# Products of a token block joined in halves of the contraction, and one rotation of eight PSUM banks for the FFN

## The chip, the cores and the metric

The kernel runs on one core of a Trainium2 chip. The time is the device time in microseconds (us) of one execution of the whole program, taken as the median of three runs. The profile shows one execution by engine: TensorE (PE, its weight loads as PEld), VectorE (DVE), ScalarE (ACT), GpSimd (POOL), and the queues of DMA issues, of which SyncE's (SP) and ScalarE's carry most here.

## The reference

One layer of a diffusion backbone: 2048 latent tokens of width 1024, and 256 context tokens beside them.

```python
n = modulate(rmsnorm(h, g), shift, scale)                 # for latent and context tokens
q, k, v, u, gate_attn, gate_ssm = split(n @ w_in)         # one in-projection
a = neighbourhood_attention(rope(q), rope(k), v, k_ctx, v_ctx, rpb)   # 8 heads of 64
s = s5_branch(u_ctx, u)                                   # bidirectional complex-diagonal scan
h = h + g1 * ((sigmoid(gate_attn) * (a @ w_branch_attn)
             + sigmoid(gate_ssm) * (s @ w_branch_ssm)) @ w_out)
h = h + g2 * swiglu(modulate(rmsnorm(h, g_ffn), sh2, sc2))  # hidden width 2816
out = rmsnorm(h, final_g)

def swiglu(h):
    a, b = split(h @ w_ffn_in)
    return (silu(a) * b) @ w_ffn_out
```

All inputs are float32. The kernel keeps float32 by splitting each operand in a high and a low part (`hi`, `lo`) and adding three products, hi x hi, hi x lo and lo x hi.

## The kernel before

**Stages.** The program runs the norm of all tokens (`norm_u`, which also stores the normalised tokens, split in two, to DRAM as `ns`), then the S5 scan and the attention with the in-projection running beside both, then the merge of the two branches, and from about 1800 us on the FFN. Tokens go in four blocks of 512.

**What sets the order.** The code is written operation by operation, and a scheduler puts the instructions of each engine in an order by priorities and by a timeline that it simulates. Code inside `hot()` has a higher priority (L64 to L66); the whole in-projection has a lower one, so that its products fill what the scan leaves. Each engine and each DMA queue then runs its own list strictly in order, and an instruction that waits holds up all behind it on its engine. Buffers come from pools with a fixed number of slots; a new tile waits for the readers of the old one.

**Weights.** `piece` (L79) loads a weight tile of 512 KB (`raw`, issued by SP at L76), lets ScalarE write its high part (`whi`, L70) and VectorE its low part (`wlo`, L71). `mm3` (L89 to L94) issues the three matmuls of one contraction tile: L92, L93 and L94.

**In-projection** (`in_proj`, L350). For blocks 1 to 3 the eight tiles of normalised tokens (`n`, each 128 x 2 x 512) are loaded from `ns` on SP's queue (L357), into a ring of 12 slots that the old block's tiles and the tables of the attention's bias (`biases`, L430, on GpSimd, in block 1) also use. A block runs the four k products (`qk`, `isk` true), v, the four q products and 2 x 8 gate products, all through `cols` (L96), which takes one weight piece at a time and adds 8 contraction tiles x 3 matmuls of 512 columns onto one PSUM bank. The pool `gpm` has two banks. The results of q and k go through rotary products on ScalarE and VectorE into `qt` (two slots, written at L397 and L398), which `store` (L362) sends out in four DMAs on SP's queue.

**FFN** (`ffn`, L1096). Each block has 11 pairs of calls of `ffn_in` (L1019), one call for the half `a` of the hidden units and one for `b`. A call computes a 256 x 512 result (two halves of the units by two halves of the tokens) by Strassen's scheme in Winograd's form: seven products of 12 matmuls each, with 256 columns (`prod`, L1063 to L1069), instead of eight. The weight side of the products is named s1, s3, s2, s4, a11, a22, a12; s1 and s3 share one split weight (`s13`), s2 and s4 another (`s24`), a11 and a22 a third (`r[0]`), and a12 has its own. The sums `s13` (block 0 only) and `s24` are made by GpSimd (L1036, L1037, L1049, L1050), and later blocks load `s13` from DRAM. The token side, `X`, has seven tiles for each of four contraction tiles.

A call has two PSUM banks, `pa` and `pb`, each with two halves of 256 columns, out of a pool of four (`fpm`). The products leave their sums there, and VectorE and ScalarE read them: L1076 copies s1's result, L1079 adds s3's to it, L1084 and L1085 read a11's and s2's, L1087 reads s4's, L1090 a22's, L1093 a12's. A wait for a bank is a wait for the readers of both of its halves.

After three or four pairs (a group) the products with `w_f2` follow (L92 to L94 by `product`, L1158): two column halves of 512, each with four token tiles `j` in four banks `pos` of their own pool `po`. In the last group of a block GpSimd and VectorE turn the sums into the output, and the next block's tokens are normalised and transposed meanwhile: `norm_ffn` (L990) has four steps, each with transposes into two banks out of `fpm`, and per step two rounds of VectorE and ScalarE work (L1010 to L1016) that make `X` out of `os`. One step is taken after each weight piece (`between`).

## Time and profile before

| | |
|---|---|
| median of three runs | 3296.73 us (3295.64 to 3303.11) |
| the profiled execution | 3294.7 us, its span 3292.9 us |
| busy share of the span | PE 95%, PEld 83%, DVE 70%, ACT 49%, POOL 27% |
| mean granted clock of TensorE | 0.983 of full |
| the chain that ended last | PE 72%, DVE 11%, DMA 9%, the rest 8% |

The span is what the trace covers; the 1.8 us around it belong to the execution. A busy share is a mean over all stages. A row of the waits says which engine and line waited, for which engine and line, how long in total, how often and how long at most. A matmul row's own length is longer than the distance to the next start, since matmuls are pipelined.

### The profile page before, as it was taken

How to read it: one execution, taken by the hardware profiler on the slowest of the kernel's cores; microseconds unless marked ns; L12 is line 12 of the kernel's file. 1: busy time of each engine (PE TensorE's matmuls, PEld its weight loads, DVE VectorE, ACT ScalarE, POOL GpSimd, SP SyncE). 2: the span in 40 equal slices, each digit the busy share in tenths (PEclk: the TensorE clock that was granted, in tenths of full speed). 3: DMA queues.
4: the chain of work that ended last, by engine and by line, in shares of the span. 5: the costliest groups of instructions: out<-in, count | busy, mean ns of one | idle time of the engine just before them, and what ended most of it. 6: DMA issues, size and time to landing. Idle time of an engine off the chain costs nothing.

```text
span 3292.9 us, 54200 instructions
## 1 busy us (share of the span) xinstructions
PE 3140.3 (95%) x20600; PEld 2738.5 (83%) x20600; DVE 2313.2 (70%) x4121; ACT 1598.6 (49%) x2778; POOL 882.4 (27%) x856
## 2 busy tenths in 40 slices
PE   8999978999899999899999999999999999999998
PEld 6987766777788778778898888889989898989988
DVE  6688787888353475565657766887869856886666
ACT  4455434554465545456553444444535543554534
POOL 2000052001232222223200444632241423442242
PEclk9999989999999999999999999999999999999999
DMA  8445566445776887786847334434344333343332
GB/s 333 171 122 168 170 203 221 164 140 165 231 210 189 243 267 231 225 261 191 259 145 243 131 129 137 138 128 144 113 139 146 121 116 130 134 149 130 107 112 100
DMA packets 212852, 564.27 MB, mean 171 GB/s; under 512 B 31784, under 2 KB 63656, under 8 KB 212592
## 3 DMA queue, kind: packets, MB, share of 16 engines
q1 hardware_dynamic: 155008, 437.48, 40.1%
q0 software_dynamic: 28032, 87.64, 9.8%
q10 hardware_dynamic: 29552, 35.70, 3.2%
q8 instruction: 162, 2.65, 0.3%
q14 instruction: 98, 0.80, 0.1%
HBM read 446.95 MB, written 111.61 MB: 170 GB/s over the span
## 4 chain that ended last, share of the span: by engine, by line
PE 72%; DVE 11%; DMA 9%; issue 3%; ACT 2%; POOL 2%; SPq 0%; ACTq 0%; DVEq 0%; POOLq 0%
PE ps L92 10%; PE ps L94 10%; PE ps L93 10%; PE ps L1067 6%; PE ps L1069 6%; PE ps L1068 6%; PE po L93 4%; PE po L92 4%; PE po L94 4%; DVE wlo L71 4%; PE o L924 3%; DMA raw<-in_w_m 2%; DMA n<-in_rpb 2%; PE w L884 2%; PE w L905 1%
## 5 line engine op out<-in xcount | busy, mean ns | idle before, releaser
L71 DVE TENSOR_TENSOR wlo<-raw,whi 128x1024 fp32r<-128x1024 f32 (+1 forms) x522 | 661.5, 1269 | 350.1 <-ACT whi L70 341.3
L70 ACT CAST whi<-raw 128x1024 fp32r<-128x1024 f32 (+1 forms) x522 | 507.6, 974 | 536.0 <-PE ps L1068 141.5
L1067 PE MATMUL ps<-X,whi 128*128 128x256 f32 x2464 | 700.0, 285 | 30.8 <-DVE u L1085 10.6
L1069 PE MATMUL ps<-X,wlo 128*128 128x256 f32 x2464 | 689.9, 285 | 10.0 <-DVE wlo L71 8.6
L1068 PE MATMUL ps<-X,whi 128*128 128x256 f32 x2464 | 694.4, 283 | 0.0
L1067 PEld LDWEIGHTS ps<-X,whi 128*128 128x128 f32 x2464 | 471.7, 191 | 42.2 <-DVE u L1085 16.2
L1069 PEld LDWEIGHTS ps<-X,wlo 128*128 128x128 f32 x2464 | 465.8, 191 | 17.9 <-DVE wlo L71 17.9
L1068 PEld LDWEIGHTS ps<-X,whi 128*128 128x128 f32 x2464 | 471.8, 191 | 1.3
L92 PE MATMUL ps<-n,whi 128*128 128x512 f32 (+1 forms) x800 | 321.5, 402 | 32.0 <-DVE t L384 17.6
L93 PE MATMUL ps<-n,whi 128*128 128x512 f32 (+1 forms) x800 | 318.4, 398 | 0.0
L94 PE MATMUL ps<-n,wlo 128*128 128x512 f32 (+1 forms) x800 | 317.5, 398 | 0.0
L93 PE MATMUL po<-wlo,zh 128*128 128x512 f32 x704 | 277.6, 394 | 0.0
L94 PE MATMUL po<-whi,zl 128*128 128x512 f32 x704 | 275.6, 394 | 0.0
L92 PE MATMUL po<-whi,zh 128*128 128x512 f32 x704 | 270.4, 394 | 0.0
L92 PEld LDWEIGHTS ps<-n,whi 128*128 128x128 f32 x800 | 152.6, 191 | 73.0 <-DVE t L384 14.7
L1049 POOL TENSOR_TENSOR os<-raw 128x512 f32<-128x512 f32 x66 | 96.2, 1457 | 391.6 <-DMA raw<-in_w_f 364.2
L1050 POOL TENSOR_TENSOR os<-raw,os 128x512 f32<-128x512 f32 x88 | 147.0, 1670 | 190.4 <-DMA raw<-in_w_f 188.2
L71 DVE TENSOR_TENSOR wlo<-os,whi 128x1024 fp32r<-128x1024 f32 x110 | 149.2, 1356 | 60.8 <-ACT whi L70 60.6
L70 ACT CAST whi<-os 128x1024 fp32r<-128x1024 f32 x110 | 115.3, 1048 | 143.8 <-POOL os L1050 41.9
L94 PEld LDWEIGHTS ps<-n,wlo 128*128 128x128 f32 x800 | 152.7, 191 | 36.3 <-issue 3.5
L93 PEld LDWEIGHTS ps<-n,whi 128*128 128x128 f32 x800 | 153.1, 191 | 33.7 <-issue 2.1
L92 PE MATMUL ps<-y,whi 128*128 128x512 f32 x384 | 157.1, 410 | 10.4 <-DVE t L968 5.1
(341 smaller groups left out, 7101.7 us busy)
## 6 DMA issues: line engine op xcount, KB each, us to landing
raw<-in_w_f SPq DMA_DIRECT2D x198, 512.0 KB
raw<-sums SPq DMA_DIRECT2D x66, 512.0 KB
raw<-in_w_gate SPq DMA_DIRECT2D x64, 512.0 KB
raw<-in_w_f SPq DMA_DIRECT2D x66, 256.0 KB
raw<-in_w_qk SPq DMA_DIRECT2D x32, 512.0 KB
gsc<-e ACTq DMA_DIRECT2D x64, 256.0 KB
raw<-in_w_m SPq DMA_DIRECT2D x32, 512.0 KB
t<-gsc SPq DMA_DIRECT2D x64, 256.0 KB
```

The costliest lines, as they stand in the source:

```text
L70: self.nc.scalar.copy(hi, x)
L71: self.nc.vector.tensor_tensor(lo, x, hi.bitcast(F32), op=ALU.subtract)
L92: mm(ps, l[0], r[0], start=first, stop=False)
L93: mm(ps, l[0], r[1], start=False, stop=False)
L94: mm(ps, l[1], r[0], start=False, stop=last)
L884: nc.tensor.matmul(slv, q[:, qs], kl, start=(n == 0), stop=(n == 1))
L924: nc.tensor.matmul(o[h, g, :, hf, :], l, r, start=(n == 0), stop=(n == nb + 1), skip_group_check=True)
L1049: nc.gpsimd.tensor_tensor(s24[:, 0], s13[:, 0], a11, op=ALU.subtract)
L1050: nc.gpsimd.tensor_tensor(s24[:, 1], a12, s24[:, 0], op=ALU.subtract)
L1067: mm(dst, a[0][:, k], xh, start=(first and k == 0), stop=False, skip_group_check=True)
L1068: mm(dst, a[0][:, k], xl, start=False, stop=False, skip_group_check=True)
L1069: mm(dst, a[1][:, k], xh, start=False, stop=(k == 3), skip_group_check=True)
```

## The change

In the in-projection, `cols` takes a number `pair`: the two products that begin there get both weights and both PSUM banks at once, and run tiles 0 to 3 of the contraction for the one and the other, then tiles 4 to 7 for the one and the other. It is used for the last two gate products of blocks 0 to 2 and for the first two k products of blocks 1 to 3.

In the FFN the four banks of `fpm` and the four of `fpo` become one rotation of eight. A call of `ffn_in` takes four of them, one for each of its sums, and uses half of each; a step of `norm_ffn` takes two, a column half of the `w_f2` products four. The products of a call are written in the order s1, s3, a11, s2, s4, a22, a12, s3's now begins its bank anew, and `fu` has three slots instead of two.

```diff
@@ -93,12 +93,24 @@
         mm(ps, l[0], r[1], start=False, stop=False)
         mm(ps, l[1], r[0], start=False, stop=last)
 
-    def cols(self, pool, src, kt, c0, n, ops, tag="ps"):
+    def cols(self, pool, src, kt, c0, n, ops, tag="ps", pair=None):
 
 
 
         nm = 8 // kt
         for c in range(n):
+            if pair is not None and c == pair:
+                f = ops[0][1]
+                ws = [self.piece(src, 0, c0 + c + i, kt) for i in range(2)]
+                pss = [pool.tile([P, ops[0][0]], F32, name=tag) for _ in range(2)]
+                for h in range(2):
+                    for w, ps in zip(ws, pss):
+                        for k in range(h * kt // 2, (h + 1) * kt // 2):
+                            self.mm3(ps, (w[0][:, k], w[1][:, k]), f(k), k == 0, k == kt - 1)
+                for i, ps in enumerate(pss):
+                    yield c + i, 0, ps
+            if pair is not None and c in (pair, pair + 1):
+                continue
             w = self.piece(src, 0, c0 + c, kt)
             for m in range(nm):
                 sl = slice(m * P, (m + 1) * P)
@@ -368,7 +380,7 @@
                         nc.sync.dma_start(dst[:, j, d, h, :, t:t + n].rearrange("i r t -> r i t"), x[p:p + 32].bitcast(F32))
 
             def qk(c0, ops, isk):
-                for jj, i, ps in self.cols(pm, I["w_qk"], KD, c0, 4, ops):
+                for jj, i, ps in self.cols(pm, I["w_qk"], KD, c0, 4, ops, pair=0 if b and isk else None):
                     with self.hot():
                         qt = ev.tile([P, 2, TB], F32R, name="qt")
                         if i:
@@ -420,7 +432,7 @@
                                               e[r * 64 + hf * 24:r * 64 + hf * 24 + 40])
             qk(0, [lat], False)
             for gi in range(2):
-                for m, _, ps in self.cols(pm, I["w_gate"], KD, gi * 8, 8, [lat]):
+                for m, _, ps in self.cols(pm, I["w_gate"], KD, gi * 8, 8, [lat], pair=6 if gi and b < NB - 1 else None):
                     g = ev.tile([P, TB], F32, name="e")
                     with self.hot():
                         nc.scalar.activation(g, ps, AF.Tanh, scale=0.5)
@@ -1057,8 +1069,7 @@
                 self.split(hi.rearrange("p a k m -> p a (k m)"), lo.rearrange("p a k m -> p a (k m)"), x)
             ops += [(hi[:, i], lo[:, i]) for i in range(x.shape[1])]
         s1, s3, s2, s4, a11, a22, a12 = ops
-        pa = pm.tile([P, 2, 256], F32, name="ps")
-        pb = pm.tile([P, 2, 256], F32, name="ps")
+        pb1, pb0, pa1, pa0 = (pm.tile([P, 2, 256], F32, name="ps")[:, 0] for _ in range(4))
 
         def prod(dst, a, x, first=True):
             for k in range(4):
@@ -1071,26 +1082,28 @@
         c = [tp.tile([P, 2, 256], F32, name="n") for _ in range(2)]
         u = up.tile([P, 256], F32, name="u")
         v = up.tile([P, 256], F32, name="u")
-        prod(pb[:, 1], s1, 3)
+        prod(pb1, s1, 3)
         with self.hot():
-            nc.scalar.copy(v, pb[:, 1])
-        prod(pb[:, 0], s3, 5, False)
+            nc.scalar.copy(v, pb1)
+        prod(pb0, s3, 5)
         with self.hot():
-            V.tensor_tensor(v, pb[:, 0], v, op=ALU.add)
-        prod(pa[:, 1], s2, 4)
-        prod(pb[:, 1], s4, 2, False)
-        prod(pa[:, 0], a11, 0, False)
+            V.tensor_tensor(v, pb0, v, op=ALU.add)
+        prod(pa0, a11, 0)
         with self.hot():
-            nc.scalar.copy(u, pa[:, 0])
-            V.tensor_tensor(u, pa[:, 1], u, op=ALU.add)
+            nc.scalar.copy(u, pa0)
+        prod(pa1, s2, 4)
+        with self.hot():
+            V.tensor_tensor(u, pa1, u, op=ALU.add)
             V.tensor_tensor(c[1][:, 1], u, v, op=ALU.add)
-            V.tensor_tensor(c[0][:, 1], pb[:, 1], u, op=ALU.add)
-        prod(pb[:, 0], a22, 6, False)
+        prod(pb1, s4, 2, False)
         with self.hot():
-            V.tensor_tensor(c[1][:, 0], pb[:, 0], u, op=ALU.add)
-        prod(pa[:, 0], a12, 1, False)
+            V.tensor_tensor(c[0][:, 1], pb1, u, op=ALU.add)
+        prod(pb0, a22, 6, False)
         with self.hot():
-            nc.scalar.copy(c[0][:, 0], pa[:, 0])
+            V.tensor_tensor(c[1][:, 0], pb0, u, op=ALU.add)
+        prod(pa0, a12, 1, False)
+        with self.hot():
+            nc.scalar.copy(c[0][:, 0], pa0)
         return [x.rearrange("p a t -> p (a t)") for x in c]
 
     def ffn(self, xs_, os, xp, tp, pm, first):
@@ -1102,11 +1115,11 @@
             ap = self.pool("fa", 4, ctx)
             wp = self.pool("fw", 4, ctx)
             hp = self.pool("fh", 1, ctx)
-            up = self.pool("fu", 2, ctx)
+            up = self.pool("fu", 3, ctx)
             os = Rotation(os, 2, self.pool("fos2", 1, ctx), 1)
             self.wr = Rotation(self.wr, 2, self.pool("fwr", 2, ctx), 2)
             self.wh = Rotation(self.wh, 3, self.pool("fwh", 1, ctx), 1)
-            po = self.pool("fpo", 4, ctx, space=PSUM)
+            pm = Rotation(pm, 4, self.pool("fpo", 4, ctx, space=PSUM), 4)
             fg = cp.tile([P, D], F32, name="fg")
             nc.sync.dma_start(fg, I["fg"].partition_broadcast(P))
             nxt = first
@@ -1163,7 +1176,7 @@
 
                     for c in range(2):
                         cs = slice(c * 512, c * 512 + 512)
-                        pos = {j: po.tile([P, 512], F32, name="po") for j in range(4)}
+                        pos = {j: pm.tile([P, 2, 256], F32, name="ps").rearrange("p a t -> p (a t)") for j in range(4)}
                         if last and end:
                             ws = [self.piece(I["w_f2"], m2, c, 2) for m2 in range(p0, p1)]
                         else:
```

The lists of TensorE show it inside a call of block 0 (`ps` are the PSUM banks, `X0` to `X3` the token side, `whi` and `wlo` the weight, whose numbers go up by four from s13 to s24, r[0] and r[1]). Before: whi_20646 is s13, whi_20650 s24 and whi_20654 r[0] of one call, whi_20781 s13 of the next. The piece begins with the end of a11.

```order
L1069 MATMUL ps_20662<-X2_17800,wlo_20655 128x256
L1067 MATMUL ps_20662<-X3_17801,whi_20654 128x256
L1068 MATMUL ps_20662<-X3_17801,whi_20654 128x256
L1069 MATMUL ps_20662<-X3_17801,wlo_20655 128x256
L1067 MATMUL ps_20663<-X0_17798,whi_20650 128x256 [waits DVE_49]
L1068 MATMUL ps_20663<-X0_17798,whi_20650 128x256
L1069 MATMUL ps_20663<-X0_17798,wlo_20651 128x256
L1067 MATMUL ps_20663<-X1_17799,whi_20650 128x256
L1068 MATMUL ps_20663<-X1_17799,whi_20650 128x256
L1069 MATMUL ps_20663<-X1_17799,wlo_20651 128x256
L1067 MATMUL ps_20663<-X2_17800,whi_20650 128x256
```

s4 goes onto ps_20663, the bank of s1 and s3, directly behind a11, and waits for VectorE (`DVE_49`): s3 was left there two products earlier (before s2 and a11), and L1079 has to have read it. After, in a call of the same block (whi_20535 is s13, whi_20539 s24, whi_20543 r[0]):

```order
L1078 MATMUL ps_20554<-X0_17798,whi_20543 128x256 [waits Activation_49]
L1079 MATMUL ps_20554<-X0_17798,whi_20543 128x256
L1078 MATMUL ps_20553<-X0_17798,whi_20539 128x256
L1079 MATMUL ps_20553<-X0_17798,whi_20539 128x256
L1080 MATMUL ps_20553<-X0_17798,wlo_20540 128x256 [waits DVE_49]
L1078 MATMUL ps_20553<-X1_17799,whi_20539 128x256
L1080 MATMUL ps_20554<-X0_17798,wlo_20544 128x256 [waits DVE_49]
L1078 MATMUL ps_20554<-X1_17799,whi_20543 128x256
L1079 MATMUL ps_20554<-X1_17799,whi_20543 128x256
L1080 MATMUL ps_20554<-X1_17799,wlo_20544 128x256
```

a11 begins behind s3 and takes turns with s2, each on a bank of its own. The place at which s4 begins:

```order
L1080 MATMUL ps_20553<-X2_17800,wlo_20540 128x256
L1078 MATMUL ps_20553<-X3_17801,whi_20539 128x256
L1079 MATMUL ps_20553<-X3_17801,whi_20539 128x256
L1080 MATMUL ps_20553<-X3_17801,wlo_20540 128x256
L1078 MATMUL ps_20551<-X0_17798,whi_20539 128x256 [waits Activation_49]
L1079 MATMUL ps_20551<-X0_17798,whi_20539 128x256
L1080 MATMUL ps_20551<-X0_17798,wlo_20540 128x256
L1078 MATMUL ps_20551<-X1_17799,whi_20539 128x256
```

s4 goes onto ps_20551, where s1 was left three products earlier, and waits for ScalarE (`Activation_49`) instead of VectorE.

In the in-projection, at the start of block 1, TensorE's list before (n_6558 to n_6565 are the block's tokens, whi_6666 the first k weight, whi_6711 the second, `py` belongs to the scan):

```order
L94 MATMUL ps_6670<-n_6562,wlo_6667 128x512
L92 MATMUL ps_6670<-n_6563,whi_6666 128x512 [waits DMAHW2_49]
L93 MATMUL ps_6670<-n_6563,whi_6666 128x512
L782 MATMUL py_3204<-cl_2916,h110_3198 128x8x16 [waits DVE_49]
L780 MATMUL py_3204<-mt_2967,ug_2890 128x8x16
L781 MATMUL py_3204<-cl_2916,h101_3151 128x8x16
L782 MATMUL py_3204<-cl_2916,h111_3201 128x8x16 [waits DVE_49]
L94 MATMUL ps_6670<-n_6563,wlo_6667 128x512
L92 MATMUL ps_6670<-n_6564,whi_6666 128x512 [waits DMAHW4_49]
L93 MATMUL ps_6670<-n_6564,whi_6666 128x512
L94 MATMUL ps_6670<-n_6564,wlo_6667 128x512
L92 MATMUL ps_6715<-n_6558,whi_6711 128x512 [waits Activation_49]
```

The first k product goes through all eight tiles before the second begins. After (whi_6672 is the second weight):

```order
L92 MATMUL ps_6676<-n_6563,whi_6666 128x512 [waits DMAHW2_49]
L93 MATMUL ps_6676<-n_6563,whi_6666 128x512
L94 MATMUL ps_6676<-n_6563,wlo_6667 128x512
L92 MATMUL ps_6677<-n_6558,whi_6672 128x512 [waits Activation_49]
L93 MATMUL ps_6677<-n_6558,whi_6672 128x512
L94 MATMUL ps_6677<-n_6558,wlo_6673 128x512 [waits DVE_49]
```

The second product begins after the first product's tile 3, and tile 4 follows only after it has gone through its own four:

```order
L92 MATMUL ps_6677<-n_6561,whi_6672 128x512
L93 MATMUL ps_6677<-n_6561,whi_6672 128x512
L94 MATMUL ps_6677<-n_6561,wlo_6673 128x512
L92 MATMUL ps_6676<-n_6564,whi_6666 128x512 [waits DMAHW3_49]
L93 MATMUL ps_6676<-n_6564,whi_6666 128x512
L94 MATMUL ps_6676<-n_6564,wlo_6667 128x512
```

So tile 4 of the new block, and each load wait behind it, stands 12 matmuls later. (What is called a tile's number here is its place among the eight, counted from 0; the scheduler has put some tiles in another order.)

SP's queue near the end of the same block (`n_7820` and `n_7821` are the first tiles of block 2, `qs` the stored q), before:

```order
L76 DMA raw_7344<-in_w_gate 128x1024 [waits DMAHW2_49,DMAHW0_49,DVE_49]
L368 DMA qs_78<-qt_7119 32x2x512 [waits DMAHW3_49,DVE_49]
L368 DMA qs_78<-qt_7119 32x2x512 [waits DMAHW4_49]
L368 DMA qs_78<-qt_7119 32x2x512
L368 DMA qs_78<-qt_7119 32x2x512 [waits DMAHW6_49]
L76 DMA raw_7378<-in_w_gate 128x1024 [waits DMAHW7_49,DMAHW1_49,DVE_49]
L357 DMA n_7820<-ns_85 128x1024 [waits DMASW1_49,DMASW0_49,Pool_49]
L357 DMA n_7821<-ns_85 128x1024 [waits DMASW6_49,DMASW7_49,DMASW5_49,DMASW4_49]
```

After:

```order
L76 DMA raw_7344<-in_w_gate 128x1024 [waits DMAHW2_49,DMAHW0_49,DVE_49]
L369 DMA n_7820<-ns_85 128x1024 [waits DMASW3_49,DMASW4_49,DMASW2_49,DMASW5_49,DMASW1_49,DMAHW3_49,DMASW0_49,Pool_49]
L380 DMA qs_78<-qt_7119 32x2x512 [waits DMAHW4_49,DVE_49]
L380 DMA qs_78<-qt_7119 32x2x512 [waits DMAHW5_49]
L380 DMA qs_78<-qt_7119 32x2x512 [waits DMAHW6_49]
L380 DMA qs_78<-qt_7119 32x2x512
L369 DMA n_7821<-ns_85 128x1024 [waits DMASW6_49,DMASW5_49,DMASW4_49]
L76 DMA raw_7378<-in_w_gate 128x1024 [waits DMAHW1_49,DVE_49]
```

The load of n_7820, which waits for GpSimd, now stands ahead of the four stores of qt_7119 and of the gate weight raw_7378.

## Rows read from the trace of the kernel before

**Rows 1.** Waits of PE, FFN: engine line waited for: us in total, times, longest

```profile
PE ps L1067 <- DVE u L1085: 10.6, 11, 3.2
PE ps L1067 <- DVE u L1079: 10.5, 11, 1.6
PE ps L1069 <- DVE wlo L71: 8.6, 13, 1.9
PE ps L1067 <- ACT u L1076: 3.8, 2, 2.1
PE ps L1067 <- DVE n L1087: 2.8, 3, 1.6
```

**Rows 2.** The same, token block 0

```profile
PE ps L1067 <- DVE u L1079: 10.2, 10, 1.6
PE ps L1069 <- DVE wlo L71: 6.1, 7, 1.9
```

**Rows 3.** Single matmuls of PE: start us, length us, what it is

```profile
2641.20 0.28 PE L1067 MATMUL ps<-X,whi 128*128 128x256 f32 x1
2641.32 0.28 PE L1068 MATMUL ps<-X,whi 128*128 128x256 f32 x1
...
2644.74 0.39 PE L92 MATMUL po<-whi,zh 128*128 128x512 f32 x1
2644.97 0.39 PE L93 MATMUL po<-wlo,zh 128*128 128x512 f32 x1
```

**Rows 4.** Stretches of one pair: us, busy (instructions) by engine, PEclk, DMA, GB/s

```profile
1973.45:1996.51 23.06, 21.16 (x170) 20.34 (x169) 21.20 (x26) 12.08 (x19) 13.41 (x8) 1.00 0.45 149
2829.99:2850.82 20.83, 20.30 (x171) 20.10 (x169) 17.68 (x25) 11.96 (x19) 7.49 (x4) 1.00 0.38 127
```

**Rows 5.** Groups of VectorE, first stretch: count, busy us, mean ns, idle before

```profile
L1126 DVE SCALAR_TENSOR_TENSOR n<-n 128x512 f32<-128x512 f32 x3 | 3.6, 1190 | 0.0
```

**Rows 6.** The same, second stretch

```profile
L71 DVE TENSOR_TENSOR wlo<-os,whi 128x1024 fp32r<-128x1024 f32 x2 | 2.4, 1220 | 0.5 <-ACT whi L70 0.5
...
L1126 DVE SCALAR_TENSOR_TENSOR n<-n 128x512 f32<-128x512 f32 x2 | 1.4, 675 | 0.0
```

**Rows 7.** Groups of ScalarE, second stretch

```profile
L70 ACT CAST whi<-os 128x1024 fp32r<-128x1024 f32 x3 | 3.2, 1052 | 3.7 <-POOL os L1050 2.5 <-PE ps L1069 1.3
```

**Rows 8.** Single matmuls of PE where block 1 ends, idle before in brackets

```profile
2577.09 0.39 PE L1067 MATMUL ps<-X,whi 128*128 128x256 f32 x1 [2.06 <-ACT u L1076]
...
2581.98 0.41 PE L1067 MATMUL ps<-X,whi 128*128 128x256 f32 x1 [3.19 <-DVE u L1085]
```

**Rows 9.** Tile os on VectorE: durations in ns, least, median, longest

```profile
L1010 DVE TENSOR_SCALAR os<-ps,A,B x32: 526/535/541, 1719.1 to 2906.5; 128x256 f32<-128x256 f32 x32
L1012 DVE TENSOR_TENSOR os<-os x32: 274/282/1377, 1720.0 to 2910.4; 128x128 f32<-128x128 f32 x32
...
L71 DVE TENSOR_TENSOR X<-os,X x32: 1072/1084/1952, 1723.9 to 2921.0; 128x896 fp32r<-128x896 f32 x32
```

**Rows 10.** Group of GpSimd, whole run

```profile
L1188 POOL TENSOR_TENSOR acc<-acc,n 128x512 f32<-128x512 f32 x28 | 40.1, 1441 | 143.6 <-DVE n L1186 143.6
```

**Rows 11.** Waits of PE, 300 to 900 us

```profile
PE ps L92 <- DMA n<-ns: 12.8, 3, 9.3
```

**Rows 12.** Single matmuls of PE at the start of block 3

```profile
865.06 0.80 PE L92 MATMUL ps<-n,whi 128*128 128x512 f32 x1 [9.30 <-DMA n<-ns]
...
868.42 0.79 PE L92 MATMUL ps<-n,whi 128*128 128x512 f32 x1 [1.72 <-DMA n<-ns]
```

**Rows 13.** A stretch behind that wait, columns as in rows 4

```profile
863.00:873.00 10.00, 6.22 (x16) 4.46 (x17) 0.44 (x1) 0.00 (x0) 0.52 (x1) 0.54 1.04 296
```

**Rows 14.** SP queue: start us, us, what is issued

```profile
507.45 0.35 SPq L76 DMA_DIRECT2D raw<-in_w_gate  x1
520.62 0.83 SPq L357 DMA_DIRECT2D n<-ns  x2
```

**Rows 15.** ScalarE, idle before in brackets

```profile
528.95 0.63 ACT L397 ACTIVATE qt<-t 128x512 fp32r<-128x512 f32 x1 [9.03 <-DMA qs<-qt]
```

## The prediction

> **What bounds the kernel now.** I read the waits of TensorE over the last stage first, then the same list for its first token block, then single issues, because the change touches two stretches and TensorE is the busiest engine of both. From 1800 us on (the FFN) TensorE's idle time has few names: four of the five that count are reads of a PSUM bank by VectorE or ScalarE (`u` on L1085, L1079 and L1076, `n` on L1087), 10.6 + 10.5 + 3.8 + 2.8 = 27.7 us in 27 waits, and the fifth is the low part of a weight, 8.6 us [rows 1]. TensorE waits there before it may add onto a bank that an earlier product left in it. Ten of the eleven waits for L1079, 10.2 us, lie in token block 0 [rows 2].
>
> What a wait really costs is read from starts. In a full run one 256-column matmul starts 0.12 us after the other and one of 512 columns 0.23 us [rows 3], while a row's own length is 0.28 and 0.39. So behind each wait of rows 1 another 0.28 - 0.12 = 0.16 us is lost that no idle column shows.
>
> Why block 0 is worse: one pair of `ffn_in` calls (168 matmuls, 168 x 0.12 = 20.2 us) takes 23.06 us there and 20.83 in block 3, and VectorE is busy for 21.20 of the one and 17.68 of the other [rows 4]. GpSimd works 13.41 us in the first pair and 7.49 in the second, and beside it VectorE's L1126 takes 1190 ns instead of 675 [rows 4 to 6]. So block 0 is close to VectorE's own limit, and the later blocks are TensorE's.
>
> Where a block ends there are two long waits, 2.06 and 3.19 us at the second such place [rows 8]; the first boundary has the same pair, since L1076's 3.8 us are just two waits and the longest for L1085 is 3.2 [rows 1]. In the in-projection TensorE waits for the normalised tokens (`n<-ns`) 12.8 us in three places [rows 11]: 9.30 and 1.72 at the last block's start [rows 12], and so 1.8 at another. Behind the long one TensorE's granted clock is 0.54 of full, so near 1.2 GHz, and the DMA engines are full [rows 13].
>
> **The change, part by part.** *FFN, order and banks.* No operation is added or taken away; the four 256-column results of a call stand in four banks instead of two. Before, the order has s3, s2, a11, then s4, which goes onto the bank whose other half s3 filled: two products (24 x 0.12 = 2.9 us) after s3's last matmul it waits for VectorE's read of s3 (L1079). In the same way a12 stands two products behind a11 and waits for L1085. Now s4 waits for ScalarE's copy of s1 alone, which lies three products back, and a22 and a12 also come three products, 4.3 us, after the results whose reads they need. The waits for L1079 are 1.02 us in the mean and 1.6 at the longest [rows 1, 2]; 1.4 us more slack takes nearly all of them, if VectorE keeps its pace.
>
> Block 0: ten waits, two in a pair, are five pairs' worth. A pair can't be faster than VectorE's 21.20 us; with 0.4 us for its own waits on TensorE I take 21.6, so 5 x (23.06 - 21.6) = 7 us gained. Bounds: 0 (the floor rises, below) and 10.2 + 10 x 0.16 = 11.8.
>
> The rest: 27.7 - 10.2 - (3.8 + 2 x 3.2 at two boundaries) = 7.3 us in 13 waits, with 13 x 0.16 = 2.1 hidden behind them, 9.4 in all. I take 7, since a few will come back as waits for a weight. Bounds: 0 and 9.4.
>
> *FFN, weights.* Supply of one weight is a ScalarE cast of 1.05 us and a VectorE subtraction of 1.22 [rows 6, 7], one behind the other 2.3 us and more where either queue is long. The tightest buffer before is that of s1 and s3: it is free after s3, and s1 of the next call stands 24 matmuls later, ahead of s4, so 2.9 us. Now five products lie between (7.2 us), and the tightest is that of a11 and a22, free after a22 and wanted after a12, s1 and s3, 4.3 us. The waits for `wlo` are 8.6 us in 13, 6.1 of them in block 0 [rows 1, 2], where both queues are longest; I take half, 4 gained. Bounds: 0 and 8.6 + 13 x 0.16 = 10.7.
>
> *FFN, boundaries.* Products of w_f2 and the transposes of the next block now take banks of the same eight. With the products of the first column half holding four, the transposes of steps 3 and 4 (of `norm_ffn`) have to wait until these four are read, one half (96 x 0.23 = 22 us) later than now. VectorE then has, in the 22 us of the second half: four evictions (0.68 each by L1126's row, 2.7), four half steps of 0.54 + 4 x 0.28 + 1.08 = 2.74 [rows 9], 11.0, and three splits of the next call, 3.7: 17.4 us. It fits with 4.7 to spare, but GpSimd's eight additions and products over the outputs, at least 1.44 us each [rows 10], 11.5 us, run in the same time, and if VectorE lost all of that the new block would start 6.8 us late; with each of its instructions at the longest of rows 9 (1.38 instead of 0.28, 1.95 instead of 1.08 us) the half steps alone are 4 x 8.0 = 32 us, and it would start 2.7 + 32 + 3.7 - 22 = 16.4 late. On the other side the waits of rows 8 (5.25 us) stand behind queues that three products of slack partly cover. Bounds for each boundary -5.6 and +16.4; the medians, nearest to most of the rows, say that the work fits, and I take 0.
>
> *In-projection.* At a boundary the last two gate products and the first two k products run half by half: both over tiles 0 to 3 of the contraction, then both over 4 to 7. The old block's tiles 0 to 3 are free 12 matmuls (2.8 us) sooner, so the four loads that reuse them issue 2.8 us sooner; the new block's tile 4 is wanted after 24 matmuls instead of 12, 2.8 us later. Together 5.6 us against 9.30: 3.7 stay. The 1.72 behind it I leave, and the 1.8 of the other boundary go: gain 5.6 + 1.8 = 7.4. Bounds: 0, as the DMA engines are full there [rows 13] and an earlier issue may not land earlier, and 12.8 plus some 2.6 for the half clock.
>
> *In-projection, SP's queue.* The order puts the first load of block 2's tokens (`n_7820`) ahead of four stores `qs<-qt` and one gate weight; before it stood behind them. It waits until the last bias head has been through GpSimd, and SP stands still from 507.8 to 520.62 us for it [rows 14]. The four stores were out before that; now they issue after 520.6. ScalarE's next-but-one `qt` needs their buffer; already now ScalarE stands 9.03 us for the later four [rows 15]. I take 3 us lost. Bounds: 0 (ScalarE stood anyway) and 9.
>
> Sum: -7 - 7 - 4 + 0 - 7.4 + 3 = -22.4 us. On the profiled execution's 3294.7 us that is 3272.3; the median of the runs is 2.0 above it, so 3274.
>
> **A rule weighed.** L1126 takes 1.8 times as long while GpSimd works (1190 against 675 ns), and over the pair VectorE is stretched by 21.20 - 17.68 = 3.5 us beside 13.41 us of GpSimd [rows 4 to 6]. The Trainium skill, "SBUF — State Buffer", section "Who interferes with whom", says that a VectorE instruction with two SBUF inputs and a GpSimd one that reads SBUF exclude each other for their whole length. By that, GpSimd's time would add nearly in full, and VectorE alone would need 17.68 + 13.41 = 31 us for a pair, more than the 23.06 that the trace has; here it shows a part of the rule, not its whole. It speaks against this change all the same, and is the second rival.
>
> **The rivals.** First, slower: the boundaries. Steps 3 and 4 now fall into one half of the last w_f2 products, beside GpSimd's work on the outputs, and VectorE's instructions there run at their longest. 3 x 16.4 = 49 us are lost against 22.4 gained: 3274 + 49 = 3323. For it: rows 9 have such instructions, and GpSimd's work on the outputs lies in this stretch; against it: the median is the short one, and VectorE has done both kinds of work in the same stretch so far. It decides from 7.5 us a boundary on. With the 6.8 us of the sum above it would be 3274 + 20 = 3294, no change that can be told.
>
> Second, block 0 keeps its pace: with less time per pair GpSimd covers more of it, VectorE's floor goes up to the 23 us of now, and the waits only change their names. The 7 us and block 0's share of the weights, 3, are lost: 3284.
>
> Third, the in-projection doesn't gain: the loads land no earlier since the DMA engines are full, and SP's standstill costs the upper bound. 7.4 + 6 us lost: 3287.
>
> **How the numbers follow.** The forecast 0.64 (3260 to 3286 by itself); the boundaries 0.12, half of it at the smaller price; block 0 0.13; in-projection 0.11. A measurement here tells about 0.2%, 6.6 us, from no change, so faster is below 3290.1 and slower above 3303.3. Faster: nearly all of the forecast and of block 0, and two thirds of the third, 0.80. Slower: the larger half of the boundaries, 0.07. Within: 0.13. The range for 8 in 10 takes in the second and third rival and the smaller price of the first; it leaves out the larger price, and below it the case in which nearly all waits of both stretches go: 3254 to 3296.
>
> **What would show it.** Right: in the FFN the waits of TensorE for `u` and `n` fall from 27.7 us below 8; a pair in block 0 takes 21 to 22 us with VectorE over 95% busy; waits for `wlo` stay below 6 us; the `n<-ns` wait at block 3's start is 3 to 5 us. Wrong: waits for X or the first `whi` above 5 us at each boundary (first rival), block 0's pair still at 23 us (second), `n<-ns` still near 11 us or a ScalarE standstill over 12 us near 516 us (third), `wlo` waits in every call on the a11 matmuls (a cover that I counted on is gone). A faster attention or merge than now would mean that the new order matters where I count nothing.

## The result and the profile after

The changed kernel takes 3246.45 us (median, 3245.33 to 3250.93) against 3296.82: ratio 0.9846, 95% interval 0.9829 to 0.9863. It gained 50 us where 22 were forecast, and lies below the range of 3254 to 3296. The profiled execution took 3247.5 us, with a span of 3245.7.

Where the time went is read from three kinds of single matmuls: the first of the FFN, the first of each block, and the last. Before, the FFN runs from

```profile
1831.48 0.28 PE L1067 MATMUL ps<-X,whi 128*128 128x256 f32 x1
...
3284.22 0.39 PE L94 MATMUL po<-whi,zl 128*128 128x512 f32 x1
```

and after, from

```profile
1818.08 0.28 PE L1078 MATMUL ps<-X,whi 128*128 128x256 f32 x1
...
3236.58 0.39 PE L94 MATMUL ps<-whi,zl 128*128 128x512 f32 x1
```

So it starts 13.4 us earlier and takes 1418.5 us instead of 1452.7, 34.2 less. (In the kernel after, lines of the in-projection and the FFN stand 12 lower: L1078 to L1080 are the matmuls, L1087 and L1090 read the results of s1 and s3, as L1076 and L1079 did.) The waits of TensorE in the FFN after, which answer to [rows 1]:

```profile
PE ps L1080 <- DVE wlo L71: 11.9, 13, 1.7
PE ps L1078 <- DVE u L1090: 7.3, 10, 1.6
PE ps L1078 <- ACT whi L70: 3.2, 3, 1.5
PE ps L1078 <- ACT u L1087: 0.8, 2, 0.4
```

The same for block 0 alone, which answers to [rows 2]:

```profile
PE ps L1080 <- DVE wlo L71: 7.0, 5, 1.7
PE ps L1078 <- DVE u L1090: 6.1, 8, 1.6
PE ps L1078 <- ACT whi L70: 0.3, 1, 0.3
```

Reads of results cost 8.1 us instead of 27.7; weights cost more than before, 15.1 us against 10.5. But all these rows together fell only from 38.2 us (36.3 of them in [rows 1]) to 23.2, by 15, and the FFN gained 34. Most of the missing half is in the same view of the weight loads (PEld). Before:

```profile
PEld ps L1069 <- DVE wlo L71: 17.9, 40, 2.1
PEld ps L1067 <- DVE u L1085: 16.2, 24, 3.4
PEld ps L1067 <- DVE u L1079: 13.6, 14, 1.8
PEld ps L1067 <- ACT u L1076: 4.2, 2, 2.3
PEld ps L1067 <- DVE n L1087: 3.5, 3, 1.8
PEld ps L1067 <- ACT whi L70: 3.4, 7, 1.3
```

After:

```profile
PEld ps L1080 <- DVE wlo L71: 15.2, 15, 1.9
PEld ps L1078 <- DVE u L1090: 10.1, 14, 1.8
PEld ps L1078 <- ACT whi L70: 3.8, 3, 1.7
PEld ps L1078 <- ACT u L1087: 1.2, 2, 0.6
```

That is 58.8 us in 90 waits before and 30.3 in 34 after: 28.5 of the 34.2. A late matmul shows idle time only once the one before it has ended by the trace, 0.28 us after its start, while the next could start after 0.12; the weight load shows the wait itself. The low part of the weights has 40 waits in this view and 13 in the other. The full amount is seen from starts alone: the distances from each 256-column matmul to the next matmul add up to 953.4 us before and 919.4 after.

The two pairs of calls that [rows 4] show, counted by matmuls, after (columns as there):

```profile
1955.67:1976.86 21.19, 20.59 (x170) 20.18 (x169) 21.12 (x25) 11.13 (x18) 12.17 (x7) 1.00 0.37 114
2790.28:2810.90 20.62, 20.32 (x171) 20.12 (x170) 19.59 (x24) 12.25 (x19) 7.66 (x5) 1.00 0.39 125
```

In block 0 this pair now takes VectorE's own time, 21.12 of 21.19 us. But it is one pair, cut at one place. The fifth, sixth, ninth and tenth pair of block 0, counted from the block's first matmul, have the most work for VectorE. They lie at 1956.82 to 2002.51 and 2091.30 to 2138.88 us before, at 1937.74 to 1983.13 and 2068.98 to 2115.66 after. Their sums, before:

```profile
sum 93.27, PE 84.62 PEld 81.34 DVE 86.05 ACT 46.75 POOL 58.50; mean PE 21.15 PEld 20.33 DVE 21.51 ACT 11.69 POOL 14.63
```

and after:

```profile
sum 92.07, PE 83.14 PEld 80.88 DVE 91.79 ACT 45.85 POOL 57.83; mean PE 20.79 PEld 20.22 DVE 22.95 ACT 11.46 POOL 14.46
```

They gained 1.2 us in all, and VectorE's busy time rose by 5.7. More than half of block 0's 10.8 us comes from its first pair and its eighth, which opens the last group: 23.94 to 20.65 us and 22.69 to 20.27.

At the start of block 2 the two waits of [rows 8], 5.25 us, became five short ones, 3.9 us (first and last):

```profile
2543.22 0.39 PE L1078 MATMUL ps<-X,whi 128*128 128x256 f32 x1 [0.40 <-ACT u L1087]
...
2556.49 0.39 PE L1080 MATMUL ps<-X,wlo 128*128 128x256 f32 x1 [1.24 <-DVE wlo L71]
```

In the in-projection the waits of TensorE from 300 to 900 us have no `n<-ns` any more, against 12.8 us in [rows 11]; the list begins:

```profile
PE ps L92 <- DVE t L396: 21.3, 8, 7.4
PE ps L92 <- ACT e L424: 17.8, 2, 11.4
PE ps L92 <- ACT e L438: 4.7, 1, 4.7
```

Other waits took their place, though: all rows of this stretch together are 51.9 us before and 52.0 after. From 900 us to the FFN's first matmul the rows fall from 33.7 to 21.5 us.

At the start of block 3 the last four loads of its tiles, which the change was to bring forward, issue 20 us later. Before:

```profile
847.83 2.42 SPq L357 DMA_DIRECT2D n<-ns  x4
```

After:

```profile
867.87 2.97 SPq L369 DMA_DIRECT2D n<-ns  x4
```

TensorE's list shows that the halves which the code writes are not there (after; ps_8938 and ps_8939 are the last two gate products of block 2, n_7820 to n_7827 its tiles):

```order
L94 MATMUL ps_8938<-n_7826,wlo_8929 128x512
L92 MATMUL ps_8938<-n_7827,whi_8928 128x512
L93 MATMUL ps_8938<-n_7827,whi_8928 128x512
L92 MATMUL ps_8939<-n_7820,whi_8934 128x512 [waits Activation_49]
```

The second product begins in the first one's last tile, so no tile is free sooner. Of the three boundaries only that behind block 0 has the gate products by halves in the list. The k products of block 3 are hardly changed either: the first one goes on to its fifth and sixth tile before the second begins, before and after, and the wait of 9.30 us in [rows 12] is for the fifth.

SP now stands still up to 524.91 us for the first load of block 2, with the stores behind it, as [rows 14] show it up to 520.62 (its queue; 16.26 us for three loads mean waits between them):

```profile
498.49 16.26 SPq L76 DMA_DIRECT2D raw<-in_w_gate  x3
524.91 0.33 SPq L369 DMA_DIRECT2D n<-ns  x1
525.33 2.13 SPq L380 DMA_DIRECT2D qs<-qt  x4
```

ScalarE waits 2.08 us for the stores, not 9.03 [rows 15]:

```profile
531.83 0.63 ACT L409 ACTIVATE qt<-t 128x512 fp32r<-128x512 f32 x1 [2.08 <-DMA qs<-qt]
```

### The profile page after: what moved, and what is told of

Its sections match the earlier page's. It is cut to its first block, busy times and chain, and to the rows that moved or that the text cites. A ratio compares the mean times of both kernels' runs of the same rounds, so it can differ in the third digit from the quotient of the medians.

```text
span 3245.7 us, 54290 instructions
## 1 busy us (share of the span) xinstructions
PE 3120.4 (96%) x20600; PEld 2728.4 (84%) x20600; DVE 2322.4 (72%) x4121; ACT 1594.5 (49%) x2778; POOL 897.1 (28%) x856
## 4 chain that ended last, share of the span: by engine, by line
PE 68%; DVE 8%; DMA 6%; issue 3%; POOL 2%; ACT 1%; SPq 0%; POOLq 0%; DVEq 0%; ACTq 0%
PE ps L92 12%; PE ps L93 12%; PE ps L94 12%; PE ps L1080 8%; PE ps L1078 8%; PE ps L1079 7%; PE o L936 3%; DVE wlo L71 3%; DMA n<-in_rpb 2%; PE w L896 2%; PE w L917 1%; PE c L898 1%; DMA raw<-in_w_gate 1%; PE c L919 1%; DMA raw<-in_w_bs 1%
## 5 line engine op out<-in xcount | busy, mean ns | idle before, releaser
L71 DVE TENSOR_TENSOR wlo<-raw,whi 128x1024 fp32r<-128x1024 f32 (+1 forms) x522 | 685.1, 1319 | 342.3 <-ACT whi L70 336.4
L1080 PE MATMUL ps<-X,wlo 128*128 128x256 f32 x2464 | 692.9, 284 | 12.0 <-DVE wlo L71 11.9
L1078 PE MATMUL ps<-X,whi 128*128 128x256 f32 x2464 | 693.3, 284 | 11.3 <-DVE u L1090 7.3
L1079 PE MATMUL ps<-X,whi 128*128 128x256 f32 x2464 | 690.1, 283 | 0.0
L1078 PEld LDWEIGHTS ps<-X,whi 128*128 128x128 f32 x2464 | 471.3, 191 | 15.6 <-DVE u L1090 10.1
L1080 PEld LDWEIGHTS ps<-X,wlo 128*128 128x128 f32 x2464 | 470.6, 191 | 15.6 <-DVE wlo L71 15.2
L1079 PEld LDWEIGHTS ps<-X,whi 128*128 128x128 f32 x2464 | 471.5, 191 | 0.5
L92 PE MATMUL ps<-n,whi 128*128 128x512 f32 (+1 forms) x800 | 320.3, 401 | 23.7 <-DVE t L396 16.8
L92 PE MATMUL ps<-whi,zh 128*128 128x512 f32 x704 | 277.1, 395 | 0.0
L94 PE MATMUL ps<-whi,zl 128*128 128x512 f32 x704 | 277.0, 394 | 0.0
L93 PE MATMUL ps<-wlo,zh 128*128 128x512 f32 x704 | 276.9, 394 | 0.0
L1061 POOL TENSOR_TENSOR os<-raw 128x512 f32<-128x512 f32 x66 | 114.1, 1729 | 389.2 <-DMA raw<-in_w_f 338.0
L1062 POOL TENSOR_TENSOR os<-raw,os 128x512 f32<-128x512 f32 x88 | 135.4, 1539 | 166.7 <-DMA raw<-in_w_f 164.8
```

The source lines that it names most:

```text
L71: self.nc.vector.tensor_tensor(lo, x, hi.bitcast(F32), op=ALU.subtract)
L92: mm(ps, l[0], r[0], start=first, stop=False)
L93: mm(ps, l[0], r[1], start=False, stop=False)
L94: mm(ps, l[1], r[0], start=False, stop=last)
L1061: nc.gpsimd.tensor_tensor(s24[:, 0], s13[:, 0], a11, op=ALU.subtract)
L1062: nc.gpsimd.tensor_tensor(s24[:, 1], a12, s24[:, 0], op=ALU.subtract)
```

## The experiments

My theory after the result: the two parts add; in the FFN it is the bank of its own for each result that pays; in the in-projection the freed tiles. All runs are against the kernel before on the same chip (its medians there lie between 3295.94 and 3297.78 us). Start and length of the FFN are from the profiled execution (first and last matmul); with TensorE's list of before up to the FFN (the kernel before, e1, e3, e4, e5, e6, e11) the start lies between 1831.0 and 1838.6 us, so a start alone can't tell a difference of less than 8 us.

| run | median us | ratio, 95% interval | FFN start, us | FFN, us |
|---|---|---|---|---|
| before | 3296.82 | | 1831.5 | 1452.7 |
| after | 3246.45 | 0.9846 (0.9829 to 0.9863) | 1818.1 | 1418.5 |
| e1 FFN part only | 3265.11 | 0.9905 (0.9890 to 0.9920) | 1838.6 | 1417.5 |
| e2 in-projection only | 3282.62 | 0.9960 (0.9945 to 0.9975) | 1819.3 | 1449.8 |
| e3 order only | 3337.01 | 1.0125 (1.0110 to 1.0140) | 1835.2 | 1492.5 |
| e4 rotation only | 3305.17 | 1.0026 (1.0015 to 1.0036) | 1831.0 | 1457.6 |
| e5 own banks, old order | 3283.18 | 0.9955 (0.9941 to 0.9968) | 1835.2 | 1439.6 |
| e6 e1 with two u slots | 3264.57 | 0.9900 (0.9887 to 0.9912) | 1831.2 | 1421.8 |
| e7 k products only | 3293.36 | 0.9993 (0.9984 to 1.0003) | 1827.8 | 1453.4 |
| e8 gate products only | 3279.13 | 0.9941 (0.9929 to 0.9953) | 1817.2 | 1453.9 |
| e9 old order in block 0 | 3242.89 | 0.9833 (0.9816 to 0.9851) | 1817.0 | 1412.9 |
| e10 gates 2 and 3 | 3290.59 | 0.9971 (0.9959 to 0.9984) | 1822.3 | 1454.7 |
| e11 gates, block 2 only | 3295.53 | 0.9992 (0.9983 to 1.0002) | 1836.7 | 1451.4 |
| e12 gates, block 0 only | 3294.46 | 0.9995 (0.9984 to 1.0006) | 1828.1 | 1456.0 |
| e13 gates 4 and 5 | 3300.23 | 1.0010 (1.0001 to 1.0019) | 1838.0 | 1452.1 |
| e14 gates 0 and 1 | 3289.39 | 0.9980 (0.9967 to 0.9993) | 1822.4 | 1451.5 |
| e15 e9 without the k pair | 3239.09 | 0.9826 (0.9812 to 0.9841) | 1815.2 | 1412.5 |

**The two parts.** e1 is the changed kernel without `pair`, e2 the kernel before with it:

```diff
-    self.cols(pm, I["w_qk"], KD, c0, 4, ops, pair=0 if b and isk else None)
-    self.cols(pm, I["w_gate"], KD, gi * 8, 8, [lat], pair=6 if gi and b < NB - 1 else None)
+    self.cols(pm, I["w_qk"], KD, c0, 4, ops)
+    self.cols(pm, I["w_gate"], KD, gi * 8, 8, [lat])
```

> The FFN part of the change alone; the in-projection as before, so TensorE's list up to the FFN is that of before. Theory (the two parts add): the FFN starts at 1831 us as before and takes 1418 us instead of 1453, as in the changed kernel, so the time is 3297 - 34 = 3263. Rival (the FFN runs faster because the in-projection leaves another state behind, for instance loads that are further ahead at its start): the FFN takes 1430 us or more and the time is 3275 or above.

> The in-projection part alone; the FFN as before. Theory: the FFN starts at 1818 us, 13 earlier, and takes 1453 as before, so 3297 - 13 = 3284, with no wait for n<-ns above 1 us. Rival (the prediction's own size: 9.3 + 1.7 + 1.8 us of waits shrink to about 5, and SyncE's queue gives back 3): the FFN starts at 1827 and the time is 3292.

Both as the theory had it: 32.2 and 14.7 us, together 46.9 of 50.4. The FFN takes what it takes in the changed kernel in e1, and nearly what it took before in e2; the rivals fall. The 3.5 us between 46.9 and 50.4 are less than these medians can tell apart.

**What in the FFN pays.** e3 keeps the two shared banks and the separate pools and takes the new written order alone (with three slots for u), e4 the rotation alone, e5 own banks and rotation with the order of before, e6 two slots for u:

```diff
# e3, against e1
-pb1, pb0, pa1, pa0 = (pm.tile([P, 2, 256], F32, name="ps")[:, 0] for _ in range(4))
+pb1, pb0, pa1, pa0 = pb[:, 1], pb[:, 0], pa[:, 1], pa[:, 0]
# e4, against before
-po = self.pool("fpo", 4, ctx, space=PSUM)
+pm = Rotation(pm, 4, self.pool("fpo", 4, ctx, space=PSUM), 4)
# e5, against e1: s1, s3, s2, s4, a11, a22, a12
# e6, against e1
-up = self.pool("fu", 3, ctx)
+up = self.pool("fu", 2, ctx)
```

> FFN: the new written order of the seven products with the two shared banks and the separate pools of before; in-projection as before. Theory (what pays is that a result has a bank of its own, so that no product waits for the reader of its neighbour): s4 still waits for the read of s3, the FFN takes 1445 to 1460 us and the time is 3290 to 3304. Rival (the order alone pays, since it moves the weights' last uses apart): the FFN takes 1425 to 1435 and the time is 3270 to 3280.

> FFN: the joint rotation of eight banks with two shared banks a call and the old order of products; in-projection as before. Theory (shared banks are what costs; the rotation only moves which bank is taken): FFN 1445 to 1455 us, time 3290 to 3299, the waits for L1079 and L1085 stay. Rival (more banks to turn through takes the 10 us that the three block boundaries lost less after the change): the boundaries gain 3 us each and the time is 3284 to 3288.

> FFN: a bank for each of the four sums out of the joint rotation, but the products written in the order of before (s1, s3, s2, s4, a11, a22, a12); in-projection as before. Theory (own banks are what pays, the order only fits them): the waits for L1079's and L1085's kind go all the same, the FFN takes 1418 to 1428 us and the time is 3265 to 3275. Rival (both are needed): a weight or a read one product behind takes the place, FFN 1435 or more, time 3282 or above.

> The FFN part alone with two slots for u and v instead of three; in-projection as before. Theory: the slots are no bound, the FFN stays within 3 us of the 1417.5 of the FFN part alone and the time is 3262 to 3268. Rival (the third slot lets VectorE and ScalarE start the next call's sums early and is part of the gain): FFN 1425 or more, time 3273 or above.

e3 went beyond both: the new written order with shared banks costs 40 us. The scheduler does not keep it. In the list s4 stands ahead of s2, one product and two matmuls behind s3 instead of two products, so it waits longer and more often for the read of s3 (there L1092), which shares its bank: 23.7 us in 26 waits, where it was 10.5 in 11. The waits for weights rise too, from 10.5 to 34.5 us. The waits of TensorE in its FFN begin:

```profile
PE ps L1080 <- DVE u L1092: 23.7, 26, 2.0
PE ps L1082 <- DVE wlo L71: 21.2, 24, 2.3
PE ps L1080 <- ACT whi L70: 13.3, 11, 2.4
```

e4 gains nothing: it is 8 us slower, above both of its forecasts, and the waits for L1079 and L1085 stay (11.7 and 10.1 us). So the rotation by itself pays nothing. The Trainium skill, "Perfetto Trace Analysis", section "Matmul Optimizations", asks that all eight banks be used. The kernel before does so in two pools of four, e4 in one rotation, and e4 is not faster. e5 came out as its rival had it, with 14 us: own banks pay in block 0 (358.9 us instead of 377.1, more than in the changed kernel with 366.3), but in blocks 1 to 3 a12 now waits for ScalarE's copy of a11 (L1095). Its waits from 2194 us on begin:

```profile
PE ps L1078 <- ACT u L1095: 24.8, 29, 1.5
```

So own banks and order pay together, and neither the rotation nor the third slot (e6: FFN 4 us longer, time the same) does. A bank for each sum without the new order is worth 14 us (e5), with it 32 (e1); the order without the banks costs 40 (e3).

**Old order in block 0.** e9 follows from e5: the old order for `b == 0`, the new one else. e15 also drops the k pair.

```diff
+if b == 0:
+    ...  # s1, s3, s2, s4, a11, a22, a12
+else:
     ...  # s1, s3, a11, s2, s4, a22, a12
```

> The changed kernel with the products of a call written in the old order (s1, s3, s2, s4, a11, a22, a12) in block 0 and in the new order in blocks 1 to 3; own banks, joint rotation and in-projection as in the change. Theory (in block 0 VectorE is the limit, and the old order asks less of it at the places where TensorE waits; in the later blocks the old order makes a12 wait for ScalarE's copy of a11): block 0 falls from 366.3 to about 359 us, the others stay at 352.5, 353.7 and 346.0, and the time is 3246 - 7 = 3239. Rival (the shorter block 0 of the run with the old order was paid back at the next boundary): 3244 to 3249.

> The kernel with the old order of products in block 0 (3242.9 us), without the halves of the first two k products; the last two gate products stay by halves. Theory (the gate pair alone gained 18 us against 15 for both, and the k pair adds nothing): 3236 to 3242. Rival (the difference of 3 us was that of two chips): 3242 to 3246.

Block 0 takes 358.8 us in e9 and 359.0 in e15, and the other blocks stay within 1.1 us, so the FFN gains 5.6 and 6.0, near the 7 expected. The time of e9, 3242.89 us, lies between its theory and its rival; that of e15 is where its theory had it. Against the runs of before on their own chips e9 gains 54.9 and e15 56.9 us, the changed kernel 50.4, with intervals that overlap: that they beat it is likely by the FFN's length, not shown by the time alone. Why the old order is better there was not tried. The traces show that block 0's waits for the low part of weights are 3.9 us in e5 and 7.0 in the changed kernel, and that VectorE is busy for 289.5 us of the block instead of 298.7.

**What in the in-projection pays.** e7 has only the k pair, e8 only the gate pair, e11 and e12 the gate pair at one boundary, and e10, e13 and e14 a gate pair at other places of the block, where it frees nothing (the diffs are cut to the argument of `cols`):

```diff
-pair=6 if gi and b < NB - 1 else None    # e8
+pair=6 if gi and b == 2 else None        # e11; e12: b == 0
+pair=2 if gi and b < NB - 1 else None    # e10; e13: 4; e14: 0
```

> In-projection: only the first two k products of blocks 1 to 3 by halves; FFN as before. Theory (what pays is the later need of the new block's tiles 4 to 7, since these are the ones that come last): the n<-ns wait at the last block's start falls from 11 us below 5 and the time is 3286 to 3290. Rival (the earlier freeing of the old block's tiles pays): the wait stays above 8 us and the time is 3294 to 3299.

> In-projection: only the last two gate products of blocks 0 to 2 by halves; FFN as before. Theory (the later need pays): the loads issue 2.8 us sooner, the n<-ns wait stays above 6 us and the time is 3290 to 3297. Rival (the earlier freeing pays): the wait falls below 4 us and the time is 3283 to 3288.

> In-projection: the last two gate products of block 2 alone by halves, before the boundary with the wait of 9.3 us; FFN as before. Theory (freed tiles): the order up to block 2 stays as before, the n<-ns wait behind it falls by 3 to 7 us, and the time is 3289 to 3294. Rival (the gain comes from what is rearranged earlier): 3294 to 3300, the wait above 9 us. A third outcome, 3284 or less, would mean that the order of the attention behind this boundary carries the gain.

> In-projection: the last two gate products of block 0 alone by halves, where the wait for n<-ns is 1.8 us; FFN as before. Theory (freed tiles): at most those 1.8 us, 3295 to 3300. Rival (another order of the scan's stretch and of all behind it): the FFN starts at 1824 us or earlier, the time is 3280 to 3290, and the idle time that goes lies behind 840 us.

> In-projection: the third and fourth product of the second eight gates of blocks 0 to 2 by halves, in the middle of a block, where no tile is freed early and none is new; FFN as before. Theory (the gain of the gate products is that of another order of the whole stretch, not of the freed tiles): the FFN starts at 1824 us or earlier and the time is 3280 to 3290, with the n<-ns wait still above 9 us. Rival (only the last two products gain, by what they free): the FFN starts at 1830 to 1838, the time is 3294 to 3300.

> In-projection: the fifth and sixth product of the second eight gates of blocks 0 to 2 by halves, where no tile is freed early; FFN as before. Theory (any edit that makes the scheduler arrange the stretch anew moves the time by some us, either way): 3280 to 3303, the change of idle time spread over the scan and the attention behind 1050 us. Rival (only what is freed at the boundary pays, and e10 was an accident): 3295 to 3300.

> In-projection: the first two products of the second eight gates of blocks 0 to 2 by halves; FFN as before. Theory (another order of the stretch): the time differs from that of the other two places by more than 3 us, within 3280 to 3303. Rival (only the boundary pays): 3295 to 3300 like the other one.

The gate pair alone gains 18 us, more than either forecast of e8; the k pair gains nothing that can be told. Neither theory is decided by this, since at the start of block 3 the edits do not reach TensorE's list. In e7 the list differs from that of before in a few dozen places, four of them at block 3's start. In e11 it is that of the kernel before, matmul for matmul: the scheduler has put the two gate products whole behind each other again. So e11 tells only what two runs of one list differ by (0.9992), and its wait stays as it must (waits of TensorE in e11, 300 to 900 us):

```profile
PE ps L92 <- DMA n<-ns: 13.2, 3, 9.5
```

In e8 these two products stand whole as well, and still the `n<-ns` waits fall from 12.8 to 9.0 us. In e12 the list has the halves behind block 0, the wait of 1.8 us there is gone, and the time is the same. So what the change gained before the FFN is not the freed tiles of the long wait; what is left is another order. In e8, e10 and e12 to e14 the pair moves hundreds of rows of TensorE's list, and the three places that free nothing gave -7, +4 and -7 us against before on the same chip. Where TensorE's idle time lies is seen from three stretches: the scan with the start of block 2's loads, the start of block 3, and the attention with the merge (columns: stretch, length, PE busy, PEclk, DMA share, GB/s). Before:

```profile
400.00:560.00 160.00, 127.97 (x705) 0.90 0.67 215
840.00:880.00 40.00, 28.98 (x116) 0.83 0.92 280
1050.00:1450.00 400.00, 369.52 (x2397) 0.96 0.81 240
```

After:

```profile
400.00:560.00 160.00, 121.16 (x639) 0.86 0.68 209
840.00:880.00 40.00, 35.32 (x168) 0.91 0.97 300
1050.00:1450.00 400.00, 379.24 (x2464) 0.97 0.82 240
```

e10:

```profile
840.00:880.00 40.00, 30.91 (x125) 0.87 0.91 282
1050.00:1450.00 400.00, 374.35 (x2475) 0.97 0.81 238
```

Idle time rises by 6.8 us in the first stretch and falls by 6.3 in the second and by 9.7 in the third, where no product by halves runs. e10 gets half of the third without a boundary; but e13 has the same 374.39 us there and is 4 us slower, so one stretch does not tell what a run gains. How much of e8's 18 us belongs to its place and how much to the order that came of it stays open: one place gave -18, three others -7 to +4, and the boundary behind block 0 taken singly (e12) nothing. The boundary behind block 1, where e8's list has the halves in part, was not tried alone.

## Why the prediction was wrong

The direction held, and in the FFN the cause did: results with banks of their own stopped waiting for each other's readers. Three terms of the FFN had a wrong size, and in the in-projection the mechanism itself was not there. By the profiled executions, forecast and measured:

| term | forecast | measured |
|---|---|---|
| FFN block 0, with 3 us of its weights | -10 | 377.1 to 366.3, -10.8 |
| FFN, starts of blocks 1 to 3 (first 252 matmuls) | 0 | 112.6 to 103.4, -9.2 |
| FFN, the rest, with 1 us of weights | -8 | -14.2 |
| up to the FFN's start | -4.4 | -13.4 |
| behind the FFN's last matmul | 0 | +0.4 |
| sum (span) | -22.4 | -47.2 |

*FFN, block 0* came out near its size, in part by luck. The step "ten waits, two in a pair, are five pairs' worth" took one pair for all. That pair went to 21.19 us, where 21.6 were expected, but the four pairs with the most work for VectorE gained 1.2 us together, because VectorE's floor rose as the second rival had it (in all of block 0 its busy time went from 291.9 to 298.7 us, while GpSimd did the same work). The gain came where VectorE was no limit, at the start of the block and of its last group.

*FFN, the rest* failed at the step "behind each wait of rows 1 another 0.28 - 0.12 = 0.16 us is lost that no idle column shows". An idle column does show it, that of the weight loads, and the 0.16 was put only on the waits that [rows 1] list; the waits shorter than that are in no row of the matmuls. The bound of 9.4 us was no bound. The weight loads' rows show 58.8 us where the matmuls' show 38.2. The Trainium skill, "Perfetto Trace Analysis", section "Identifying the Most-Contended Engine", says that matmul busy time judges TensorE badly and the weight loads' busy share well. Here the trace agrees, in the idle time before them: 15 us of change in the one and 28.5 in the other.

*FFN, weights*: the step "I take half, 4 gained" expected more time between the uses of each buffer to halve the waits for the low part. In the matmuls' rows these waits rose from 8.6 to 11.9 us, and 11 of the 13 stand before a11, the sign that the text had named as wrong. In the weight loads' rows they fell from 17.9 to 15.2. The supply cost more than the text took for it. In the 11 waits before a11 the buffer had long been free; the subtraction that fills it began with no idle time of VectorE before it, in eight of them right behind another weight's subtraction, and in these it took 1.96 to 1.99 us, not the 1.22 of [rows 6] (VectorE's rows around the wait at 1856.19 us, with another of its instructions left out):

```profile
1851.93 1.99 DVE L71 TENSOR_TENSOR wlo<-os,whi 128x1024 fp32r<-128x1024 f32 x1
...
1854.17 3.65 DVE L71 TENSOR_TENSOR wlo<-raw,whi 128x1024 fp32r<-128x1024 f32 x2
```

The second row is two such subtractions. So VectorE's queue set the time there, and the buffers, which the text counted, did not.

*FFN, boundaries*: the step "the medians, nearest to most of the rows, say that the work fits, and I take 0" chose between -5.6 and +16.4 by the work of the moved steps, and that work hid itself (no wait for `X` appears); what counted was that the reads at the block's start no longer stand in the way. The first rival is refuted by these starts.

*In-projection*: the step that failed is "the old block's tiles 0 to 3 are free 12 matmuls (2.8 us) sooner, so the four loads that reuse them issue 2.8 us sooner; the new block's tile 4 is wanted after 24 matmuls instead of 12". It took the halves from the code. At the boundary with the 9.30 us TensorE's list has neither: the gate products stand one behind the other, the first k product goes through its fifth tile first, and the loads issue 20 us later, not 2.8 sooner. The start of block 1, from which the halves were read, shows it too: `n_6563`, behind which the second k product begins, is the sixth tile and not the fourth, and before the change the second product already began ahead of the first one's eighth tile. The `n<-ns` waits went altogether, 12.8 us, and other waits came in their place, so that TensorE's waits from 300 to 900 us add up to as much as before. For SP's queue 3 us were counted as lost. ScalarE waits 2.08 us where it was looked for, not 9 to 12; what the standstill costs elsewhere is not shown, but TensorE's idle time from 400 to 560 us, where it lies, rose by 6.8. What was left out is the time behind 900 us, where the waits fell by 12 us of the 13.4; the text names the attention at its end as the sign that "the new order matters where I count nothing". The forecast had no term for it, and one run of a changed order can't give one: three such orders spread over 11 us.

## What to carry to other kernels

Where matmuls follow each other faster than their rows are long, count waits in the rows of the weight loads; the matmuls' own idle time hid half of what this change was worth. Two results that share a bank share their waits, so give each its own bank before the products are put in another order: the new order written without them cost 40 us here, and with them it was worth 18 more. Where a scheduler orders the program, an edit also moves what it doesn't touch, by -7 to +4 us here: put the same edit at a place where it can't help before its gain is put down to a mechanism, and read the scheduled list of a run before believing that it tests what its edit says: e11's list was that of the kernel before.

## What was not expected of the hardware

The same GpSimd instruction takes longer after the change. The group on the page of before:

```profile
L1049 POOL TENSOR_TENSOR os<-raw 128x512 f32<-128x512 f32 x66 | 96.2, 1457 | 391.6 <-DMA raw<-in_w_f 364.2
```

and on the page of after:

```profile
L1061 POOL TENSOR_TENSOR os<-raw 128x512 f32<-128x512 f32 x66 | 114.1, 1729 | 389.2 <-DMA raw<-in_w_f 338.0
```

The mean of 66 went from 1457 to 1729 ns, and that of VectorE's low parts from 1269 to 1319. A faster FFN alone does not go with it: in e5, whose FFN is 13 us shorter than before, the mean is 1519 ns, in e4, whose FFN is 5 us longer, 1591, and in e1, with own banks and the new order, 1757. Spans on GpSimd are rough, and no run was made to tell why.
